# Up projection of a decoder layer: halo columns in four of seven Strassen parts, and the second half's halo read from the first half's result

## The chip, the cores and the metric

The kernel runs on one core of one Trainium2 chip. The metric is device time in microseconds (us) of one execution, from the first to the last instruction and what lies around them. Inside the core TensorE (PE) multiplies matrices, VectorE (DVE) and ScalarE (ACT) work on elements, GpSimd (POOL) is nearly unused here, and SyncE (SP) issues most DMAs. SBUF is the memory that the engines read, PSUM the one that TensorE writes its sums to.

## The reference

One layer of a hybrid decoder: 16 meta tokens and 1024 tokens, model width 1024, feed-forward width 2816. Attention and a convolution branch are merged, projected and normalized to `h`; then comes the convolutional feed-forward, which is where the change is:

```python
h  = layer_norm(DEEPNORM_ALPHA * h + mixed @ W_out)
up = causal_dwconv(h @ ffn_w_up, ffn_dw, ffn_dw_b)      # 1024 -> 2*2816, FFN_TAPS = 3
u, g = jnp.split(up, 2, axis=-1)
f  = (jax.nn.gelu(g, approximate=False) * u) @ ffn_w_down
h  = layer_norm(DEEPNORM_ALPHA * h + f)                 # meta tokens dropped
```

The convolution is causal with three taps, so each output token needs the up projection of its own token and of the two before it. A piece of tokens that is convolved by itself needs two columns more on its left: its halo.

## The kernel before, in words

**Stages.** Input projection, attention and convolution branch, merge, output projection (`out_rows`, which also normalizes `h` and turns it so that channels lie on partitions), up projection with convolution and gate, down projection. Every product is done in three terms, high part by high part, high by low and low by high, on operands split into two rounded fp32r halves. A split is two instructions: ACT casts to the high half, DVE subtracts to get the low half.

**The up projection as Strassen.** The 1024 tokens are cut into a first half (tokens 0 to 511) and a second half (512 to 1023), the 1024 input channels and the 2 x 2816 output channels also in two each. One product by halves is then seven products instead of eight, on seven sums of the inputs. In the order in which they are used these are B11, B21, BT2, BT4, BT1, BT3, B22. Each half of tokens is again done in two sub-halves of 256 columns: `sub` 0, whose operand has two more columns on its left, the halo, and `sub` 1. In `sub` 0 column 0 and 1 stand for tokens -2 and -1 in the first half, and for tokens 510 and 511 in the second. One part in one sub-half is 12 matmuls: four blocks `k` of 128 input channels by three terms. In `sub` 0 eight of the 12 are 260 columns wide (two columns of low halo, two of high halo, 256 tokens: the halo's low half lies ahead of its high half in the same row, so that a separate term isn't needed), the other four are 256 wide. In `sub` 1 all are 256 wide.

**The loop.** `for c in range(FC)` goes over 22 chunks of 128 + 128 output channels (the u side `c` and the gate side `FC + c`). The parts accumulate in four PSUM tiles: px, pz, px, pw, py, px, py for the seven parts in their order. After a part, `copy` (ACT) or `tt` (DVE) takes the bank to SBUF and forms the four Strassen results c11 and c12 (the gate's two token halves), c21 and c22 (u's two halves); u13 and u2 are intermediate sums. These are 516 columns wide: two columns of low halo product, two of high, 512 tokens. `conv_ffn` first adds the two halo products with two one-column activations on ACT, then convolves (one ACT instruction, two DVE instructions); `gelu` and `f_out` make the gate and store the product. Chunk 0 is done in two passes, `sub` 1 first and then `sub` 0, because the last rows of `h` come late: between the two passes `turn` transposes and evicts the last rows, and the sums of the parts of `sub` 0 (`form_t2`, `form_t3`, `form_t4`) and their splits (`bsplit` by `split_of`) are formed. `edges` puts the halo of both halves into the first two columns of each channel block of `h` in the tile FA, from the small tile `edge`, which `turn` fills.

**Order.** Each engine works its own queue in the order in which the instructions were given or ranked (`rank`, `after`, `line` pin some of them). Weights are loaded by SP, split by `wsplit` up to nine products ahead (`w_ahead(9)`), and kept in a ring in RHO and in the tiles `w`.

**Where operands lie.** Buffers come from pools on two sides of SBUF. `edge` is a tile of [128 partitions, 2, 8, 2] floats, 128 bytes in each partition, on the left side. The left buffers that are allocated behind it, each one where the last one ends, are among others the weight tiles `wr` and `w`, the tiles FA, RHC, RHO, OB and OA. RX, RW and OC lie on the right side. `B_AT` says where each part's operand is: in `sub` 0 B11 in RHC, B21 in RHO, BT2, BT1, BT3 and BT4 in OA, B22 in RX; in `sub` 1 B11, B21, BT2 and BT1 in OC, the others in RHC. The weights (the operand that TensorE holds) are in RHO and `w`, in this stage and in others, and the earlier stages pair the same left and right buffers.

Of the kernel before, what the change touches and what calls it, by code (L numbers as in the profile page):

```python
# [23 lines left out]
F = mybir.dt.float32  # L24
# [89 lines left out]
def tile_hybrid_layer(  # L114
# [24 lines left out]
    @contextmanager  # L139
    def rank(p):  # L140

        saved = tc.cur_priority
        tc.cur_priority = p
        yield
        tc.cur_priority = saved
# [1088 lines left out]
            [(OC, OC_UP + i * 2048, 0) for i in range(4)] + [(RHC, x + R_DN, 0) for x in (4096, 2048, 6144)]]  # L1234
    B11, B21, BT2, BT1, BT3, BT4, B22 = range(7)

    def bsum(sub, q, hl):
        r = row(sub, q, hl)
        return r[:, :, 2:260] if sub == 0 and not hl else r

    def row(sub, q, hl):
        t, o, back = B_AT[sub][q]
        hi = HP if sub == 0 else 256
        o += (4 * 256 if back and not hl else 4 * hi if hl and not back else 0)
        n = 256 if hl else hi
        return t[:, o:o + 4 * n].rearrange("p (k n) -> p k n", k=4)

    def bmat(sub, q, j, k):

        if sub:  # L1250
            return row(1, q, j % 2)[:, k]
        return row(0, q, j % 2)[:, k, 0:(260, 256, 260)[j]]

    lined, high = [], []
# [10 lines left out]
    def wide(x):  # L1265
        return x.rearrange("p (k n) -> p k n", k=4)
# [3 lines left out]

    def bsplit(sub, q, src, cs=slice(None)):
        with rank(RK_SUMS):
            src = wide(src)[:, :, cs]
            hi = bsum(sub, q, 0)[:, :, cs]
            ins = nc.scalar.copy(hi, src)
            if (sub, q) in ((0, BT2), (0, BT4), (0, BT1), (0, BT3)):
                if high:
                    after(ins, high[-1])
                high.append(ins)
            n = src.shape[2]  # L1280
            a = cs.start or 0
            x = 2 if sub == 0 and a == 0 else 0
            a -= 2 if sub == 0 and a else 0
            lo = bsum(sub, q, 1)[:, :, a:a + n - x]
            line(nc.vector.tensor_tensor(lo, src[:, :, x:], f32(hi)[:, :, x:], OP.subtract))
            if x:
                line(nc.vector.tensor_tensor(row(0, q, 0)[:, :, 0:2], src[:, :, :2], f32(hi)[:, :, :2], OP.subtract))
# [28 lines left out]


    WO_ORDER = (4, 5, 0, 1, 2, 3, 6, 7)
    edge = const.tile([P, 2, KC, 2], F, name="edge")
    r_next = [1]  # L1320

    def out_rows(i, between=(), work=()):
# [51 lines left out]
    def turn(i, r, n, ins, banks=None, behind=None, upper=False):  # L1374
        with rank(RK_TURN):
            for j, k0 in enumerate((4, 0) if upper else (0, 4)):
                ps = banks[j] if banks else pat.tile([P, 512], F, name="ps_h", tag="s", bufs=2)
                for k in range(4):
                    ins = nc.tensor.transpose(ps[:, k * P:(k + 1) * P], r[:, (k0 + k) * P:(k0 + k + 1) * P], ident)
                    if behind:  # L1380
                        after(ins, behind[-1])
                        behind.append(ins)
                for k in range(k0, k0 + 4):
                    src = ps[:, (k - k0) * P:(k - k0) * P + n]
                    if n < P:
                        dst = edge[:, 0, k]
                    else:
                        h, jj = divmod(i, 4)
                        sub = 0 if jj < 2 else 1
                        a = 2 + jj * P - SUB[sub][0]  # L1390
                        dst = h1F(sub, h, k)[:, a:a + P]
                    nc.scalar.activation(dst, src, AF.Identity, bias=b1col(k), scale=g1col(k))
                    if i == 3:
                        nc.scalar.activation(edge[:, 1, k], src[:, P - 2:P], AF.Identity, bias=b1col(k), scale=g1col(k))
        return behind[-1] if behind else None


# [68 lines left out]
            w_ahead(n)  # L1466

    def edges():
        for h in range(2):
            with rank(RK_TURN):  # L1470
                nc.vector.tensor_copy(FA[:, h * 2064:h * 2064 + 2064].rearrange("p (k n) -> p k n", n=258)[:, :, 0:2],
                                      edge[:, h])

    ahead = []
    work = {0: [(split_of, 1, B11), (split_of, 1, B21), (split_of, 1, B22)],
# [36 lines left out]
    c11, c21, u2 = (FA[:, 4128 + i * CU:4128 + (i + 1) * CU] for i in range(3))  # L1512
    c12, c22, u13 = (RT[:, i * CU:(i + 1) * CU] for i in range(3))

    def conv_ffn(cc, o):
        t = ftmp()
        for i in range(2):
            nc.scalar.activation(cc[:, 2 + i:3 + i], cc[:, 2 + i:3 + i], AF.Identity, bias=cc[:, i:i + 1], scale=1.0)
        cc = cc[:, 2:]
        nc.scalar.activation(t, cc[:, 2:HW], AF.Identity, bias=ffw(3, o), scale=ffw(2, o))  # L1520
        nc.vector.scalar_tensor_tensor(t, cc[:, 1:HW - 1], ffw(1, o), t, OP.mult, OP.add)
        nc.vector.scalar_tensor_tensor(t, cc[:, 0:HW - 2], ffw(0, o), t, OP.mult, OP.add)
        return t

    def gelu(t):
        nc.scalar.activation(t, t, AF.Gelu)
        return t

    def f_out(c, h, gate, t):
        nc.vector.tensor_tensor(t, t, gate, OP.mult)  # L1530
        f_stores.append(load(fd[c, :, h * 512:(h + 1) * 512], t))
# [39 lines left out]
    for c in range(FC):  # L1571
        V4, X, Z, Y = (pup.tile([P, 1024], F, name=n, tag=n) for n in ("pw", "px", "pz", "py"))
        passes = ((1,), (0,)) if c == 0 else ((0, 1),)
        for subs in passes:
            last = subs == passes[-1]
            w_next = iter(range(7))
            a, b = SUB[subs[0]][0] + (2 if subs[0] else 0), SUB[subs[-1]][1] + 2

            def at(t):
                return t[:, 252 + a:252 + b]  # L1580

            def prod(q, bank, first):
                if last:
                    w_ahead(9)
                    ah, al = w_ready.pop(0)
                else:
                    ah, al = w_ready[next(w_next)]
                for sub in subs:
                    terms = [(k, j) for k in range(4) for j in range(3)]
                    if sub == 0:  # L1590
                        terms = [(k, j) for j in (0, 2, 1) for k in range(4)]
                    for i, (k, j) in enumerate(terms):
                        o = bank[:, 512:768] if sub else bank[:, (252, 256, 252)[j]:512]
                        ins = nc.tensor.matmul(o, (ah, ah, al)[j][:, k * P:(k + 1) * P], bmat(sub, q, j, k),  # L1594
                                               start=first and i == 0, stop=i == 11, skip_group_check=not first)
                        if i == 0 and last_mm:
                            after(ins, last_mm[-1])
                    last_mm.append(ins)

            def tt(*x):  # L1600
                with rank(RK_CHAIN):
                    return nc.vector.tensor_tensor(*x)

            def copy(*x):
                with rank(RK_CHAIN):
                    copied.append(nc.scalar.copy(*x))  # L1606

            prod(B11, X, True)
            copy(u13[:, a:b], at(X))
            prod(B21, Z, True)  # L1610
            if last and c not in (0, FH + 1):
                sums_load(c - 1 if c <= FH else c - 2)
            tt(c11[:, a:b], at(Z), u13[:, a:b], OP.add)
            prod(BT2, X, False)
            copy(u2[:, a:b], at(X))
            if not last:
                turn(5, *last_rows, (V4, Z), last_mm, True)
                for q in (B11, B21):
                    split_of(0, q, LATE)
                form_t2(0, LATE)  # L1620
                formed.append(lined[-1])
                form_t4(0, LATE)
                form_t3(0, LATE)
                for q in (BT2, BT4, BT1, BT3, B22):
                    split_of(0, q)
            if last:
                g0 = gelu(conv_ffn(c11, FC + c))
            prod(BT4, V4, True)
            prod(BT1, Y, True)
            copy(c22[:, a:b], at(Y))  # L1630
            prod(BT3, X, False)
            copy(u13[:, a:b], at(X))
            ins = tt(c22[:, a:b], c22[:, a:b], u13[:, a:b], OP.add)
            if last and c not in (0, FH + 1):
                sums_form(c - 1 if c <= FH else c - 2, ins)
            tt(c21[:, a:b], u13[:, a:b], at(V4), OP.subtract)
            prod(B22, Y, False)
            tt(c12[:, a:b], at(Y), u2[:, a:b], OP.add)
            if last:
                f1 = conv_ffn(c22, c)  # L1640
                f_out(c, 0, g0, conv_ffn(c21, c))
                f_out(c, 1, gelu(conv_ffn(c12, FC + c)), f1)
    up_stack.close()


# [247 lines left out]
```

## Time and profile before

| what | value |
|---|---|
| median of 3 runs | 1254.46 us (1253.59, 1254.46, 1257.59) |
| span of the profiled execution | 1253.2 us, 23194 instructions |
| TensorE busy | 1239.1 us, 99% of the span |
| VectorE busy | 1078.1 us, 86% |
| ScalarE busy | 627.4 us, 50% |
| mean granted TensorE clock | 0.999 of full speed |
| DMA | 212.20 MB, mean 169 GB/s |

The execution's own time has no row beside its span in the page; the fastest run is 0.4 us above the span, the median 1.3 us. In the profile a line such as L1594 is a line of the kernel. A row of a timeline has start, duration, engine, line, operation, output and inputs, tile on the array, shape, and the count of equal instructions in a row. Matmuls overlap: one row's end lies after the next row's start, so durations of single matmuls are longer than their spacing, and what a group costs is read from start to start.

### The profile page before, as it was taken

The page shows a single profiled execution, that of the slowest core. Times are in us where ns is not written, and L with a number is a line of the kernel's source. Part 1 is how long each engine was busy: PE and PEld are TensorE (multiplying, and loading weights), DVE is VectorE, ACT ScalarE, POOL GpSimd, SP SyncE. Part 2 cuts the span into 40 slices and gives each one's busy share as a digit, 9 for nine tenths or more (in the row PEclk, how much of TensorE's full clock was granted, in tenths as well). Part 3 has the DMA queues.
Part 4 walks back from the last instruction along what each step waited for, and adds up shares of the span by engine and source line. Part 5 has one row for each costly group of instructions (what it writes and reads, how often), then busy time and mean ns, then how long its engine had stood idle before and what let it go on. Part 6 is the DMA issues. An engine that isn't in the chain of part 4 may idle for free.

```text
span 1253.2 us, 23194 instructions
## 1 busy us (share of the span) xinstructions
PE 1239.1 (99%) x9176; PEld 1173.8 (94%) x9176; DVE 1078.1 (86%) x1862; ACT 627.4 (50%) x1284; POOL 7.4 (1%) x8
## 2 busy tenths in 40 slices
PE   8999999999999999999999999999999999999997
PEld 7999999999999999788899999999999998888886
DVE  8989999999978677448899999998999977896697
ACT  8533255655474233344676556565565654545330
POOL 0000000001000000000000000000000000000000
PEclk9999999999999999999999999999999999999999
DMA  7383633432256564222145555453454567998712
GB/s 261 117 292 102 191 93 98 109 95 81 73 157 173 170 164 119 85 94 75 68 160 191 194 197 201 161 211 137 163 206 175 196 227 251 395 342 330 276 60 84
DMA packets 98687, 212.20 MB, mean 169 GB/s; under 512 B 11395, under 2 KB 38595, under 8 KB 98322
## 3 DMA queue, kind: packets, MB, share of 16 engines
q1 hardware_dynamic: 84414, 199.57, 46.9%
q10 hardware_dynamic: 14164, 11.15, 2.8%
q8 instruction: 72, 1.18, 0.4%
q14 instruction: 37, 0.30, 0.1%
HBM read 150.29 MB, written 62.70 MB: 170 GB/s over the span
## 4 chain that ended last, share of the span: by engine, by line
PE 96%; DVE 2%; ACT 1%; DMA 1%; issue 0%; SPq 0%; DVEq 0%; ACTq 0%
PE px L1594 15%; PE py L1594 10%; PE ps_x L1739 9%; PE ps_z L340 8%; PE ps_z L343 8%; PE ps_z L344 8%; PE ps_z L1739 7%; PE ps_p L1172 7%; PE pz L1594 5%; PE pw L1594 5%; PE ps_w L344 2%; PE ps_w L343 2%; PE ps_w L340 2%; PE ps_z L575 2%; PE ps_t L943 1%; PE ps_s L919 1%
## 5 line engine op out<-in xcount | busy, mean ns | idle before, releaser
L340 PE MATMUL ps_z<-RHO,w 128*128 128x256 f32 (+2 forms) x864 | 243.2, 281 | 0.0
L343 PE MATMUL ps_z<-RHO,w 128*128 128x256 f32 (+2 forms) x864 | 242.3, 280 | 0.0
L344 PE MATMUL ps_z<-RHC,w 128*128 128x256 f32 (+2 forms) x864 | 242.2, 280 | 0.0
L343 PEld LDWEIGHTS ps_z<-RHO,w 128*128 128x128 f32 x864 | 162.5, 188 | 0.5
L344 PEld LDWEIGHTS ps_z<-RHC,w 128*128 128x128 f32 x864 | 162.7, 188 | 0.2
L340 PEld LDWEIGHTS ps_z<-RHO,w 128*128 128x128 f32 x864 | 162.5, 188 | 0.1
L749 DVE SCALAR_TENSOR_TENSOR FA<-cin,cdw,FA 128x1026 f32<-128x1026 f32 x120 | 154.3, 1295 | 0.7
L300 ACT CAST w<-wr 128x1024 fp32r<-128x1024 f32 x37 | 38.8, 1048 | 64.0 <-PE ps_z L344 48.0
L1412 DVE TENSOR_TENSOR RHO<-wr,RHO 128x512 fp32r<-128x512 f32 x94 | 64.0, 684 | 3.6 <-ACT RHO L1411 3.5
L1411 ACT CAST RHO<-wr 128x512 fp32r<-128x512 f32 x94 | 56.9, 619 | 15.6 <-DVE wr L1429 7.9
L1429 DVE TENSOR_TENSOR wr<-wr 128x512 f32<-128x512 f32 x88 | 60.1, 683 | 0.1
L758 ACT ACTIVATE FA<-ps_z,colr 128x258 f32<-128x258 f32 (+1 forms) x64 | 30.1, 472 | 59.0 <-PE ps_z L344 50.7
L303 DVE TENSOR_TENSOR w<-wr,w 128x1024 fp32r<-128x1024 f32 x37 | 45.1, 1218 | 7.6 <-ACT w L300 7.4
L1606 ACT COPY FA<-px 128x516 f32<-128x516 f32 (+2 forms) x23 | 13.1, 571 | 71.2 <-PE px L1594 71.2
L1172 PE MATMUL ps_p<-OC,w 128*128 128x256 f32 (+1 forms) x384 | 48.1, 278 | 0.0
L1172 PE MATMUL ps_p<-OA,w 128*128 128x256 f32 (+1 forms) x384 | 47.8, 278 | 0.0
L1172 PEld LDWEIGHTS ps_p<-OC,w 128*128 128x128 f32 x384 | 46.2, 188 | 0.1
L1172 PEld LDWEIGHTS ps_p<-OA,w 128*128 128x128 f32 x384 | 45.9, 188 | 0.0
L1412 DVE TENSOR_TENSOR w<-wr,w 128x512 fp32r<-128x512 f32 x60 | 40.7, 684 | 4.7 <-ACT w L1411 4.7
L1594 PE MATMUL px<-OA,RHO 128*128 128x260 f32 x324 | 43.0, 282 | 0.0
L1594 PE MATMUL px<-OC,RHO 128*128 128x256 f32 x324 | 41.2, 276 | 0.8 <-DVE OB L1345 0.8
L1594 PE MATMUL px<-RHC,RHO 128*128 128x256 f32 (+1 forms) x312 | 40.6, 279 | 0.1
(457 smaller groups left out, 3109.3 us busy)
## 6 DMA issues: line engine op xcount, KB each, us to landing
wr<-in_w_up_dram SPq DMA_DIRECT2D x44, 512.0 KB, 3.6
wr<-in_w_z_dram SPq DMA_DIRECT2D x29, 512.0 KB, 4.2
OB<-in_w_down_dram SPq DMA_DIRECT2D x24, 512.0 KB, 5.2
fd<-FA SPq DMA_DIRECT2D x44, 256.0 KB, 2.0
FA<-sd SPq DMA_DIRECT2D x15, 512.0 KB, 8.9
qt<-qd SPq DMA_DIRECT2D x28, 256.0 KB, 4.1
OB<-td SPq DMA_DIRECT2D x14, 512.0 KB, 8.7
sgd<-FA ACTq DMA_DIRECT2D x48, 128.0 KB, 2.4
```

What stands on the lines that cost most here:

```text
L300: ins = nc.scalar.copy(hi, raw)
L303: return nc.vector.tensor_tensor(lo, raw, f32(hi), OP.subtract)
L340: ins = nc.tensor.matmul(ps, al, bh, start=i == 0, stop=False)
L343: nc.tensor.matmul(ps, ah, bh, start=False, stop=False)
L344: last = nc.tensor.matmul(ps, ah, bl, start=False, stop=i == n - 1)
L749: nc.vector.scalar_tensor_tensor(acc[c], cin[:, j:j + U], wc, acc[c], OP.mult, OP.add)
L1172: nc.tensor.matmul(ps[:, :b - a], x, rhs(k, hl, a, b), start=k + j == 0, stop=k == 3 and j == 2)
L1411: nc.scalar.copy(hi, src)
L1412: ins = nc.vector.tensor_tensor(lo, src, f32(hi), OP.subtract)
L1429: ins = nc.vector.tensor_tensor(*x)
L1594: ins = nc.tensor.matmul(o, (ah, ah, al)[j][:, k * P:(k + 1) * P], bmat(sub, q, j, k), start=first and i == 0, stop=i == 11, skip_group_ch ...
L1739: nc.tensor.matmul(banks[i], l[:, ts], r[:, ws], start=first and a and x + k == 0, stop=z and x == len(ops) - 1 and k == 2, skip_group_che ...
```

## The change

Four parts, B11, B21, BT3 and BT4, keep the halo in `sub` 0 (`HALO`). BT2, BT1 and B22 have none any more: all their 12 matmuls are 256 wide, in the order of `sub` 1's terms, on an operand without the halo in front. In Strassen's sums these three parts enter u2, c22 and c12. Hence u2, c22 and c12 are copied and added from column 4 on, and their halo columns are not computed at all: the convolution of c22 and c12 (second half of the tokens) gets its two halo columns by one ACT copy of the last two columns of c21 and c11 (first half), which are those very tokens. c11 and c21 (first half) still use the two activations, on products of parts with halo. For the four parts to give the first half's halo without the three others, `edges` now sets the halo of the four quadrants of `h` (by half and channel block) to E0, E1, E0 and 0, where E are the two edge tokens of the first half: the sums of the three dropped parts would be zero there. The second half's edge is not needed, so that `edge` is [P, KC, 2], 64 bytes in each partition, and the eight activations of `turn` that filled the other half are gone. The splits of the three parts cast 1024 columns instead of 1032, and lose their DVE subtraction of the halo's low part.

The diff (the line numbers of the profile are those of the kernel before; what stands below line 1234 moves by up to 14 lines):

```diff
+    HALO = (B11, B21, BT3, BT4)
+
     def bsum(sub, q, hl):
         r = row(sub, q, hl)
+        if sub == 0 and not hl and q not in HALO:
+            t, o, back = B_AT[0][q]
+            o += back * 1024
+            return t[:, o:o + 1024].rearrange("p (k n) -> p k n", k=4)
         return r[:, :, 2:260] if sub == 0 and not hl else r
...
         if sub:
             return row(1, q, j % 2)[:, k]
+        if q not in HALO:
+            return (row(0, q, 1) if j == 1 else bsum(0, q, 0))[:, k]
         return row(0, q, j % 2)[:, k, 0:(260, 256, 260)[j]]
...
     def bsplit(sub, q, src, cs=slice(None)):
         with rank(RK_SUMS):
-            src = wide(src)[:, :, cs]
+            whole = sub == 0 and q not in HALO
+            src = wide(src)[:, :, slice(2, None) if whole else cs]
...
-            x = 2 if sub == 0 and a == 0 else 0
+            x = 2 if sub == 0 and a == 0 and not whole else 0
...
-    edge = const.tile([P, 2, KC, 2], F, name="edge")
+    edge = const.tile([P, KC, 2], F, name="edge")
...
-                    if i == 3:
-                        nc.scalar.activation(edge[:, 1, k], src[:, P - 2:P], AF.Identity, bias=b1col(k), scale=g1col(k))
...
     def edges():
-        for h in range(2):
-            with rank(RK_TURN):
-                nc.vector.tensor_copy(FA[:, h * 2064:h * 2064 + 2064].rearrange("p (k n) -> p k n", n=258)[:, :, 0:2],
-                                      edge[:, h])
+        with rank(RK_TURN):
+            halo = FA[:, 0:2 * 2064].rearrange("p (k n) -> p k n", n=258)[:, :, 0:2]
+            nc.vector.tensor_copy(halo[:, 0:KC], edge)
+            nc.vector.tensor_copy(halo[:, KC:KC + 4], edge[:, 0:4])
+            nc.vector.memset(halo[:, KC + 4:], 0.0)
...
-    def conv_ffn(cc, o):
+    def conv_ffn(cc, o, before=None):
         t = ftmp()
-        for i in range(2):
-            nc.scalar.activation(cc[:, 2 + i:3 + i], cc[:, 2 + i:3 + i], AF.Identity, bias=cc[:, i:i + 1], scale=1.0)
+        if before is not None:
+            nc.scalar.copy(cc[:, 2:4], before[:, HW:CU])
+        else:
+            for i in range(2):
+                nc.scalar.activation(cc[:, 2 + i:3 + i], cc[:, 2 + i:3 + i], AF.Identity, bias=cc[:, i:i + 1],
+                                     scale=1.0)
...
-                    if sub == 0:
+                    if sub == 0 and q in HALO:
                         terms = [(k, j) for j in (0, 2, 1) for k in range(4)]
                     for i, (k, j) in enumerate(terms):
-                        o = bank[:, 512:768] if sub else bank[:, (252, 256, 252)[j]:512]
+                        o = bank[:, 512:768] if sub else bank[:, (252 if q in HALO and j != 1 else 256):512]
...
-            copy(u2[:, a:b], at(X))
+            copy(u2[:, m:b], at(X, m))
...
-            copy(c22[:, a:b], at(Y))
+            copy(c22[:, m:b], at(Y, m))
...
-            ins = tt(c22[:, a:b], c22[:, a:b], u13[:, a:b], OP.add)
+            ins = tt(c22[:, m:b], c22[:, m:b], u13[:, m:b], OP.add)
...
-            tt(c12[:, a:b], at(Y), u2[:, a:b], OP.add)
+            tt(c12[:, m:b], at(Y, m), u2[:, m:b], OP.add)
             if last:
-                f1 = conv_ffn(c22, c)
+                f1 = conv_ffn(c22, c, c21)
                 f_out(c, 0, g0, conv_ffn(c21, c))
-                f_out(c, 1, gelu(conv_ffn(c12, FC + c)), f1)
+                f_out(c, 1, gelu(conv_ffn(c12, FC + c, c11)), f1)
```

**TensorE in chunk 1, before.** The seven parts of `sub` 0 (260 wide, from RHC, RHO, OA, RX) take turns with those of `sub` 1 (256 wide, from OC and RHC); the first name is the PSUM tile, the names behind the arrow are where the two operands lie. Here stand BT2 to BT1 with the `sub` 1 groups between them.

```order
L1594 MATMUL px<-OA,RHO 128x260 x8
L1594 MATMUL px<-OA,RHO 128x256 x4
L1594 MATMUL px<-OC,RHO 128x256 x12
L1594 MATMUL pw<-OA,RHO 128x260 x8
L1594 MATMUL pw<-OA,RHO 128x256 x4
L1594 MATMUL pw<-RHC,RHO 128x256 x12
L1594 MATMUL py<-OA,RHO 128x260 x8
L1594 MATMUL py<-OA,RHO 128x256 x4
L1594 MATMUL py<-OC,RHO 128x256 x12
```

The same place of the changed kernel.

```order
L1608 MATMUL px<-OA,RHO 128x256 x12
L1608 MATMUL px<-OC,RHO 128x256 x12
L1608 MATMUL pw<-OA,RHO 128x260 x8
L1608 MATMUL pw<-OA,RHO 128x256 x4
L1608 MATMUL pw<-RHC,RHO 128x256 x12
L1608 MATMUL py<-OA,RHO 128x256 x12
L1608 MATMUL py<-OC,RHO 128x256 x12
```

BT2 (px) and BT1 (py) lose the eight wide matmuls, BT4 (pw) keeps them; the number of matmuls and their order among parts is the same.

**ScalarE between the two passes of chunk 0, before.** The last rows' transposes are evicted (L1392), then the parts of `sub` 0 are cast (L1275), with weight casts (L1411) and copies out of PSUM (L1606) among them.

```order
L1392 ACTIVATE FA<-pz,colr 128x128 x4
L1275 CAST RX<-FA 128x4x258
L1411 CAST w<-wr 128x512
L1411 CAST RHO<-wr 128x512
L1606 COPY OB<-py 128x256
L1275 CAST OA<-OB 128x4x258
L1411 CAST RHO<-wr 128x512
L1606 COPY OB<-px 128x256
L1275 CAST OA<-FA 128x4x258 x3
L1606 COPY OB<-px 128x260
```

The same place of the changed kernel.

```order
L1401 ACTIVATE FA<-pz,colr 128x128 x4
L1526 COPY OB<-FA 128x2
L1284 CAST RX<-FA 128x1024
L1418 CAST w<-wr 128x512
L1418 CAST RHO<-wr 128x512
L1620 COPY OB<-py 128x256
L1284 CAST OA<-OB 128x1024
L1418 CAST RHO<-wr 128x512
L1620 COPY OB<-px 128x256
L1284 CAST OA<-FA 128x4x258
L1284 CAST OA<-FA 128x1024
L1284 CAST OA<-FA 128x4x258
L1620 COPY OB<-px 128x260
```

The two-column copy of chunk 0's first halo (L1526, from c11 in FA to c12 in OB) now stands at the head of this stretch, since its source is ready from the first pass; three of the five casts are 8 columns narrower.

More of the change, by code (lines that the diff above doesn't have):

```diff
@@ L1385, in turn @@
                     if n < P:
-                        dst = edge[:, 0, k]
+                        dst = edge[:, k]
                     else:
@@ L1577, in tile_hybrid_layer, with at @@
             a, b = SUB[subs[0]][0] + (2 if subs[0] else 0), SUB[subs[-1]][1] + 2
-            def at(t):
+            m = max(a, 4)
+            def at(t, a=a):
                 return t[:, 252 + a:252 + b]
```

## The prediction

> **What bounds the kernel now.** I read the page's busy times and its chain of waits first, then the busy times by stage, then the timeline of TensorE through one chunk.
>
> ```profile
> PE 1239.1 (99%) x9176; PEld 1173.8 (94%) x9176; DVE 1078.1 (86%) x1862; ACT 627.4 (50%) x1284; POOL 7.4 (1%) x8
> PE 96%; DVE 2%; ACT 1%; DMA 1%; issue 0%; SPq 0%; DVEq 0%; ACTq 0%
> ```
>
> TensorE is busy for 99% of the span and makes 96% of the chain. By stage (stretch, length, then busy time of PE, weight load, DVE, ACT, POOL, granted clock, DMA share, GB/s):
>
> ```profile
> 602.00:640.00 38.00, 35.98 (x299) 34.86 (x298) 34.79 (x63) 25.58 (x53) 0.00 (x0) 1.00 0.22 80
> 640.00:1034.00 394.00, 394.00 (x3400) 394.00 (x3399) 363.74 (x578) 236.46 (x504) 0.00 (x0) 1.00 0.52 189
> ```
>
> The second row is the up projection's steady part: TensorE never idles, at clock 1.00. The first is its entry, where TensorE idles 38.00 - 35.98 = 2.0 us. So in the loop only a shorter or longer stream of matmuls moves the end, as long as DVE (394.00 - 363.74 = 30.3 us idle) and ACT keep up. One period of the stream, TensorE's timeline from BT1 (py) of one chunk to BT1 of the next:
>
> ```profile
> 773.70 1.58 PE L1594 MATMUL py<-OA,RHO 128*128 128x260 f32 x12
> 775.11 1.52 PE L1594 MATMUL py<-OC,RHO 128*128 128x256 f32 x12
> 776.47 1.59 PE L1594 MATMUL px<-OA,RHO 128*128 128x260 f32 x12
> ...
> 779.26 1.59 PE L1594 MATMUL py<-RX,RHO 128*128 128x260 f32 x12
> 780.69 1.52 PE L1594 MATMUL py<-RHC,RHO 128*128 128x256 f32 x12
> 782.05 1.59 PE L1594 MATMUL px<-RHC,RHO 128*128 128x260 f32 x12
> ...
> 787.62 1.59 PE L1594 MATMUL px<-OA,w 128*128 128x260 f32 x12
> 789.05 1.52 PE L1594 MATMUL px<-OC,w 128*128 128x256 f32 x12
> ...
> 793.18 0.40 PE L1594 MATMUL py<-OA,w 128*128 128x260 f32 x2
> ```
>
> Costs are read from start to start. A group of 12 with halo ("128x260") takes 775.11 - 773.70 = 1.41 us as BT1, 1.43 as B22 (780.69 - 779.26) and 1.43 as BT2 (789.05 - 787.62). A group of 12 at 256 takes 1.36 (776.47 - 775.11, 782.05 - 780.69), or 1.36 / 12 = 113.3 ns each.
>
> **The change, part by part.** *Narrower matmuls.* The three parts lose 0.05 + 0.07 + 0.07 = 0.19 us per chunk, on the path: 22 x 0.19 = 4.2 us gained, if they then run like the 256 wide groups of today. One rule speaks for less: the Trainium skill (TensorE: Matmul & The Clock Gate, Back-to-back issue gap) gives an isolated spacing of N / 2.4 + 2.5 ns, so four columns are 1.7 ns, and 24 matmuls in 22 chunks an estimated 0.9 us. The rows show four times that, since the wide groups cost more than their columns, and they decide.
>
> *Halo by copy.* Two pairs of one-column activations per chunk become two copies of two columns. Pairs on ACT's timeline:
>
> ```profile
> 627.24 0.48 ACT L1518 ACTIVATE OB<-OB 128x1 f32<-128x1 f32 x2
> 627.62 0.80 ACT L1520 ACTIVATE FA<-OB,coll 128x512 f32<-128x512 f32 x1
> ```
>
> A pair takes 627.62 - 627.24 = 0.38 us, so one instruction 0.19; ACT gains some 0.38 us per chunk. It is 40% idle in the steady stretch (236.46 of 394.00), so this is worth nothing. The copy for c22 waits for c21, and the one for c12 for c11. Those sums come one and many instructions earlier on the same DVE queue, and behind the waiting copies stand only convolutions whose results go out by DMA, so nothing that TensorE needs soon. The narrower copies and additions (512 for 516 columns) are too small to count.
>
> *Halo splits.* Three of the seven subtractions of L1287 go:
>
> ```profile
> 619.89 0.15 DVE L1287 TENSOR_TENSOR OA<-FA,OA 128x8 fp32r<-128x8 f32 x1
> 619.97 1.21 DVE L1285 TENSOR_TENSOR OA<-FA,OA 128x1024 fp32r<-128x1024 f32 x1
> ```
>
> 0.08 us from start to start, three times 0.24 us once in the kernel, on DVE between the two passes. The waits of TensorE there end on ACT, not on these, so I count nothing; at most it gains 0.24. The eight edge activations that go run earlier, under the output projection, and are hidden by it.
>
> *One instruction moved on ACT.* Between the passes of chunk 0 the copy of the halo columns of c12 comes ahead of the casts of the last parts. That place is a queue that TensorE waits for:
>
> ```profile
> 610.23 1.53 ACT L1392 ACTIVATE FA<-pz,colr 128x128 f32<-128x128 f32 x4
> 611.62 1.09 ACT L1275 CAST RX<-FA 128x1032 fp32r<-128x1032 f32 x1
> ...
> 613.60 0.42 ACT L1606 COPY OB<-py 128x256 f32<-128x256 f32 x1
> 613.87 1.11 ACT L1275 CAST OA<-OB 128x1032 fp32r<-128x1032 f32 x1
> ...
> 615.34 0.42 ACT L1606 COPY OB<-px 128x256 f32<-128x256 f32 x1
> 615.61 3.02 ACT L1275 CAST OA<-FA 128x1032 fp32r<-128x1032 f32 x3
> 618.48 0.43 ACT L1606 COPY OB<-px 128x260 f32<-128x260 f32 x1
> ```
>
> From 610.23 to 618.9 ACT has no gap. The two copies out of px, at 615.34 and 618.48, free the bank for the next part. TensorE (rows below) starts at 615.82, 1.73 us after the 12 of 614.09, which take 1.36, and at 618.96, right after the copy's end:
>
> ```profile
> 614.09 1.66 PE L1594 MATMUL py<-RHC,w 128*128 128x256 f32 x12
> 615.82 1.70 PE L1594 MATMUL px<-RHC,RHO 128*128 128x260 f32 x12
> 617.35 1.59 PE L1594 MATMUL pz<-RHO 128*128 128x260 f32 x12
> 618.96 1.71 PE L1594 MATMUL px<-OA,RHO 128*128 128x260 f32 x12
> ```
>
> An instruction of 0.19 us at the queue's head delays both by 0.19; since the first delay already shifts TensorE, it is paid once. The three casts lose 8 of 1032 columns, together some 0.02. I take +0.17; its ends are 0 (if the copy slips into an earlier gap) and 0.4 (if an instruction with a cold start takes the 0.3 to 0.4 us that a row shows from start to end and the second wait adds its own).
>
> *Sum of these.* -4.2 + 0.17 = -4.0 us. Against the profiled span of 1253.2 that is 1249.2; the median of the runs stands 1.3 above the span, so 1254.46 - 4.0 = 1250.4.
>
> *Addresses.* `edge` falls from 128 to 64 bytes, so all left buffers allocated behind it (`wr`, `w`, FA, RHC, RHO, OB, OA) move down by 64 bytes, while RX, RW and OC on the right stay. Each matmul that takes its moving columns from the right and its weights from the left gets another distance between its two addresses. In the up projection these are the 256 wide groups from OC (four parts) and B22's from RX: 5 x 12 = 60 per chunk, 1320 in all. Nothing in the trace of before shows that distance change. What it does show is that matmuls of the same shape and buffers run at two speeds (merge stage):
>
> ```profile
> 485.56 1.52 PE L1172 MATMUL ps_p<-OC,w 128*128 128x256 f32 x12
> 486.92 1.41 PE L1172 MATMUL ps_p<-OA,w 128*128 128x256 f32 x11
> ...
> 502.66 0.39 PE L344 MATMUL ps_w<-OA,RHC 128*128 128x512 f32 x1
> 502.89 2.99 PE L1172 MATMUL ps_p<-OC,w 128*128 128x256 f32 x24
> 505.71 0.40 PE L340 MATMUL ps_w<-OA,RHC 128*128 128x512 f32 x1
> ```
>
> Twelve from OC take 486.92 - 485.56 = 1.36 us, 113.3 ns each. Twenty-four a little later, behind 512 wide ones of another product, take 505.71 - 502.89 = 2.82, 117.5 ns each. No wait stands in these rows; TensorE just runs 4.2 ns slower per matmul and doesn't recover within 24. So matmul and weight load, both busy without a gap, can be in step or out of it, and the step depends on how the streams meet. I take it that the distance of the addresses is part of that. The price is bounded by 0 (no effect) and 4.2 ns on every matmul whose distance changes. Of the two ends I take the upper, since the row that shows a lost step is the only one here that prices it: 1320 x 4.2 = 5.5 us in this stage. In other stages the same holds for the merge's products from OC (the page's L1172 row of 384 of them: 1.6 us) and for some 600 matmuls of 512 columns that pair RX, RW or OC with left weights (by the same 4.2 ns 2.5 us, at the lower end 0). Sum: 5.5 + 1.6 + 2.5 = 9.6 us lost, against 4.0 gained: 1254.46 + 5.6 = 1260.1.
>
> **The rivals.** *A, the streams keep step.* The sum without the addresses: 1250.4, and faster. For it: every group of 256 in the period above, from OC, RHC, `w` or RHO, takes the same 1.36, although OC, RHC, `w` and RHO lie in different places; and the stream recovers from each wide group within the next one. Against it: those distances have been the same all through before, so the equality proves little, and the 117.5 exists. The Trainium skill (SBUF, Who interferes with whom) says that TensorE reads moving columns and weights through independent ports and never waits on anyone, which speaks for A: by it the addresses cost nothing. The two speeds of one and the same matmul above are not covered by that rule, and I take the rows as evidence that it isn't the whole.
>
> *B, a change of distance costs only its transition.* BT2, BT1 and B22 now have another spacing of rows (256 for 264 columns), and part follows part in other distances; each switch costs a few ns and then the stream is in step again. A wide group shows the size of such a switch: 8 matmuls of 260 with 4 of 256 cost 0.05 to 0.07 more than 12 of 256, of which the columns themselves explain 8 x (4 / 256) x 113.3 = 14 ns, so 36 to 56 ns for two switches, 18 to 28 each. With the 3 x 2 switches saved and, per chunk, 5 to 6 new ones, 5 x 18 to 6 x 28 ns, 2.0 to 3.7 us are given back in 22 chunks, and some more in the merge: 1252.4 to 1255, say 1254, no change that can be told.
>
> *D, ACT's queue decides.* If the copies for c22 and c12 made ACT wait long enough for the weights' casts behind them to come late, TensorE would stall in each chunk. TensorE idles nowhere in the steady stretch, and splits run up to nine products (about 9 x 2.8 us) ahead, so a wait of a few us is absorbed. It decides only when such a wait passes some 6 us per chunk, and the additions that the copies wait for come within one or two parts. From there each us more costs 22 us. I give it 2 in 100.
>
> The point from which C, the forecast, turns the sign: 4.0 us over the 2300 matmuls in question is 1.7 ns each. Below that the kernel is faster, at 3.4 ns it is slower by 0.3%.
>
> **How the numbers follow.** C (addresses lose the step) 0.48, A 0.34, B 0.16, D 0.02. A measurement of this kernel tells 0.3% from no change (its three runs lie within 0.32%), that is 1250.7 and 1258.2. C gives 1256 (a price half as high) to 1267 (all 136 matmuls of 256 columns of a chunk out of step: 22 x 76 x 4.2 = 7.0 us more); 1256 to 1258.2 is the same, about 0.08 of its 0.48. A gives 1249.4 (the wide groups' after-effects go too) to 1251, two thirds of it under 1250.7: faster 0.24, with 0.04 of B for 0.28. The same: 0.10 of A, 0.10 of B, 0.08 of C, 0.28. Slower: 0.40 of C, 0.02 of B, 0.02 of D, 0.44. The likeliest is C, 1260.1, its own range 1256 to 1267. The range over the cases is 1249.2 to 1266, which leaves out D, the worst of C and the best of A.
>
> **What would show it.** C: in the profile after, groups of 256 from OC take 1.41 us from start to start where those from RHC take 1.36, and merge rows from OC show 117.5. A: all groups of 256, BT2, BT1 and B22 among them, take 1.36, and a period is 19.48 - 0.19 = 19.29 us. B: 256 wide groups between 1.37 and 1.40, of all sources. The moved copy: the copies out of px end 0.17 later against the last eviction of the transposes, and TensorE's second wait with them. D: rows of TensorE with idle time in the steady stretch, ended by ACT. Wrong in any case would be a period above 19.9 us, or an idle TensorE there, or another granted clock.

## The result and the profile after

The changed kernel takes 1263.43 us (median; 1263.26 to 1266.32), the kernel before 1254.79 beside it. The ratio is 1.0076, 95% interval 1.0064 to 1.0087: slower by 0.8%. The forecast was slower, 1260.1 in a range of 1249.2 to 1266. The page's busy times and the engines of the chain of waits:

```profile
PE 1249.3 (99%) x9176; PEld 1181.6 (93%) x9176; DVE 1076.3 (85%) x1860; ACT 613.1 (48%) x1232; POOL 7.4 (1%) x8
PE 96%; DVE 2%; ACT 1%; DMA 1%; issue 0%; SPq 0%; DVEq 0%; ACTq 0%
```

TensorE has as many matmuls as before (9176), 3 parts x 8 x 22 = 528 of them four columns narrower, and is busy for 10.2 us more. DVE and ACT work less. The steady stretch of the up projection, columns as before (stretch, length, busy time of PE, weight load, DVE, ACT, POOL, clock, DMA share, GB/s):

```profile
640.00:1034.00 394.00, 394.00 (x3359) 394.00 (x3359) 361.64 (x577) 223.53 (x461) 0.00 (x0) 1.00 0.51 183
```

In the same 394 us TensorE still never idles, at the same clock, but comes to 3359 matmuls instead of 3400. Nothing waits, the stream itself is slower. TensorE's timeline in the changed kernel shows where:

```profile
773.23 1.58 PE L1608 MATMUL pz<-OC,w 128*128 128x256 f32 x12
774.65 1.58 PE L1608 MATMUL px<-OA,RHO 128*128 128x256 f32 x12
776.07 1.59 PE L1608 MATMUL px<-OC,RHO 128*128 128x256 f32 x12
777.49 1.60 PE L1608 MATMUL pw<-OA,RHO 128*128 128x260 f32 x12
778.93 1.53 PE L1608 MATMUL pw<-RHC,RHO 128*128 128x256 f32 x12
780.29 1.52 PE L1608 MATMUL py<-OA,RHO 128*128 128x256 f32 x12
781.65 1.58 PE L1608 MATMUL py<-OC,RHO 128*128 128x256 f32 x12
783.07 1.60 PE L1608 MATMUL px<-OA,RHO 128*128 128x260 f32 x12
...
785.87 1.60 PE L1608 MATMUL py<-RX,RHO 128*128 128x256 f32 x12
787.31 1.52 PE L1608 MATMUL py<-RHC,RHO 128*128 128x256 f32 x12
788.67 1.59 PE L1608 MATMUL px<-RHC,RHO 128*128 128x260 f32 x12
...
792.95 1.58 PE L1608 MATMUL pz<-OC,w 128*128 128x256 f32 x12
```

From start to start a group from OC takes 774.65 - 773.23 = 1.42 us, 783.07 - 781.65 = 1.42; before it was 1.36. A group from RHC still takes 1.36 (780.29 - 778.93, 788.67 - 787.31). Of the three parts that lost the halo only BT1 (py from OA) comes to 1.36; BT2 (px from OA) takes 776.07 - 774.65 = 1.42, hardly less than with the halo, and B22 (py from RX) 787.31 - 785.87 = 1.44, more than with it. The period is 792.95 - 773.23 = 19.72 us, before 19.48. The merge shows the same split by source, 1.42 us for 12 from OC, 118.3 ns each, and 1.26 for 11 from OA, 114.5; over the whole stage the 256 wide rows from OC go from 113.8 to 118.8 ns, and those from OA, which take turns with them, from 113.4 to 115.9:

```profile
489.00 1.58 PE L1172 MATMUL ps_p<-OC,w 128*128 128x256 f32 x12
490.42 1.43 PE L1172 MATMUL ps_p<-OA,w 128*128 128x256 f32 x11
491.68 1.58 PE L1172 MATMUL ps_p<-OC,w 128*128 128x256 f32 x12
```

Summed from start to start over all matmuls of a stage, after against before: merge 90.61 against 88.64 (+2.0), output projection 89.82 against 89.13 (+0.7), up projection 434.83 against 429.58 (+5.2), down projection 211.09 against 209.46 (+1.6), together 9.5 us. The rest of the difference of the two profiled spans (1264.5 - 1253.2 = 11.3) lies nearly all in the first stage, where matmuls wait for the first loads; that part differs between profiles whatever the kernel (one line's matmuls there, L518, take 9.3 to 11.9 us in the four profiles of the kernel before, the changed one and the first two experiments). The profile of the changed kernel is of its longest run (1266.32); the medians differ by 8.6.

### The profile page after: what moved, and what is told of

The parts are those of the page before. It is cut to its first block, busy times and chain, and to the rows that moved or that the text cites. A ratio compares the mean times of both kernels' runs of the same rounds, so it can differ in the third digit from the quotient of the medians.

```text
span 1264.5 us, 23150 instructions
## 1 busy us (share of the span) xinstructions
PE 1249.3 (99%) x9176; PEld 1181.6 (93%) x9176; DVE 1076.3 (85%) x1860; ACT 613.1 (48%) x1232; POOL 7.4 (1%) x8
## 4 chain that ended last, share of the span: by engine, by line
PE 96%; DVE 2%; ACT 1%; DMA 1%; issue 0%; SPq 0%; DVEq 0%; ACTq 0%
PE px L1608 15%; PE py L1608 9%; PE ps_x L1753 9%; PE ps_z L340 8%; PE ps_z L343 8%; PE ps_z L344 8%; PE ps_p L1172 7%; PE ps_z L1753 7%; PE pz L1608 5%; PE pw L1608 5%; PE ps_w L340 2%; PE ps_w L344 2%; PE ps_w L343 2%; PE ps_z L575 2%; PE ps_t L943 1%; PE ps_z L572 1%
## 5 line engine op out<-in xcount | busy, mean ns | idle before, releaser
L1620 ACT COPY FA<-px 128x512 f32<-128x512 f32 (+1 forms) x23 | 13.1, 568 | 81.0 <-PE px L1608 81.0
L1608 PE MATMUL px<-OA,RHO 128*128 128x256 f32 (+1 forms) x324 | 42.9, 281 | 0.0
L1532 ACT ACTIVATE FA<-OB,coll 128x512 f32<-128x512 f32 x44 | 35.8, 815 | 13.8 <-DVE OB L1616 13.8
```

## The experiments

**Take the address shift out of the change.** One line of the changed kernel:

```diff
-    edge = const.tile([P, KC, 2], F, name="edge")
+    edge = const.tile([P, 2, KC, 2], F, name="edge")[:, 0]
```

> The changed kernel, with the edge tile kept at 128 bytes (half of it unused), so that all buffers lie where they lay before; nothing else differs. Theory C (addresses): the groups of 256 from OC are back at 1.36 us from 1.42, the merge's rows from OC back at the spacing of before, and the whole comes to 1251 to 1253 us, faster than before. Rival (the narrower parts and their order disturb the stream wherever the buffers lie): OC groups stay at 1.42 and the time at 1262 to 1264.

Measured: 1253.78 us (11 runs), ratio 0.9993, interval 0.9984 to 1.0002. The slowdown is gone with 64 unused bytes. The profile (TensorE):

```profile
780.58 1.56 PE L1608 MATMUL py<-RX,RHO 128*128 128x256 f32 x12
781.98 1.53 PE L1608 MATMUL py<-RHC,RHO 128*128 128x256 f32 x12
...
787.55 1.52 PE L1608 MATMUL pz<-OC,w 128*128 128x256 f32 x12
788.91 1.56 PE L1608 MATMUL px<-OA,w 128*128 128x256 f32 x12
790.32 1.53 PE L1608 MATMUL px<-OC,w 128*128 128x256 f32 x12
```

OC is back at 1.36 (788.91 - 787.55). The time, though, is a little above the 1251 to 1253 that was expected: B22 takes 1.40 (781.98 - 780.58) and BT2 1.41 (790.32 - 788.91), not 1.36. So part of the gain from the narrower matmuls was still missing, and the interval allows no difference from before: the slowdown is gone, but the expected "faster" is not shown.

**The address shift alone.** The kernel before, with 16 floats of padding in a small tile ahead of the left buffers taken away, so that they lie 64 bytes lower, and no other edit:

```diff
-    coll = const.tile([P, n_kept - n_right + 24], F, name="coll")[:, :n_kept - n_right]
+    coll = const.tile([P, n_kept - n_right + 8], F, name="coll")[:, :n_kept - n_right]
```

> The kernel before, with 64 bytes of padding ahead of the left buffers taken away, so that they lie 64 bytes lower, as in the changed kernel; no instruction differs. Theory C: OC groups of 256 go from 1.36 to 1.42 (4 x 22 x 0.06 = 5.3 us), the merge loses 2 us, the other stages some 2, together 1263 to 1266 us. Rival (addresses don't matter): 1254 to 1256, all groups as before.

Measured: 1265.69 us, ratio 1.0090, interval 1.0075 to 1.0106. Not one instruction differs from the kernel before. By the starts of the matmuls the OC groups take 1.42 us in all 21 full chunks (1421 ns on average), the merge is at 90.61 us as in the changed kernel, and the up projection 7.1 us longer. The address shift alone is enough for the whole slowdown. By the sums of the starts the up projection loses 7.1 us with it and 5.2 with the change, so the narrower matmuls gave 1.8 back; the intervals of the two ratios overlap.

**What the spacing depends on.** Matmuls alone, in place of the layer:

```python
for wi in range(8):
    for mi in range(8):
        run(f"n_{LET[mi]}{LET[wi]}", mi * 8, wi * 8, 256, 256, 3)   # start of moving columns, of weights; width, spacing of rows, repeats
...
```

> A kernel of matmuls alone, which leaves the whole layer out: streams of 36 matmuls 256 wide, fp32r, with the order of terms of one part, for each of 8 x 8 pairs of start addresses of moving columns and weights (steps of 32 bytes, letters a to h), then 260 wide ones in the halo's row spacing, then 512 wide ones. Theory C: the spacing depends on the distance of the two addresses; some pairs at 113.3 ns, some at 117 to 120, and pairs of the same distance agree. Rival: 113.3 ns for all 64 pairs.

Measured, mean spacing of the last 12 of each 36, by the distance "address of the weights minus address of the moving columns, modulo 256 bytes" (eight pairs for each, the first pair at 0 bytes, n_aa, 119.4, ran while the stream started):

| distance, bytes | 0 | 32 | 64 | 96 | 128 | 160 | 192 | 224 |
|---|---|---|---|---|---|---|---|---|
| 256 wide, ns | 119.4 to 120.0 | 118.4 to 118.7 | 113.3 (one: 117.8) | 117.1 to 119.0 | 118.2 to 118.8 | 120.0 | 117.8 | 117.8 |
| 512 wide, ns | 227.2 to 230.6 | 232.5 to 232.8 | 232.5 to 233.3 | 233.7 to 234.6 | 232.8 to 233.6 | 233.0 to 234.5 | 228.5 to 229.7 | 233.2 to 233.5 |

From 60 to 480 us of that kernel VectorE, ScalarE and GpSimd do nothing, and the granted clock is 1.00. The 260 wide streams in the halo's row spacing, in which the distance moves on by 32 bytes with every block, come to 119.2 to 121.1 ns at all eight starts. Four neighbouring streams on its timeline, second letter the weights, first letter the moving columns, each letter 32 bytes on:

```profile
67.10 4.39 PE L40 MATMUL n_gb<-M,W 128*128 128x256 f32 x36
71.33 4.28 PE L40 MATMUL n_hb<-M,W 128*128 128x256 f32 x36
75.44 4.40 PE L40 MATMUL n_ac<-M,W 128*128 128x256 f32 x36
79.68 4.42 PE L40 MATMUL n_bc<-M,W 128*128 128x256 f32 x36
```

n_hb (distance 64 modulo 256) takes 75.44 - 71.33 = 4.11 us, n_gb (96) 4.23, and n_ac 4.24, although its distance is 64 as well: it is the one exception, taken up below. The rival, 113.3 for all pairs, falls. In the kernel before, the addresses that its program assigns give 64 for all groups of 256 in merge and up projection, and 0 for the 512 wide matmuls of output and down projection: the best place of each row of the table. In the changed kernel, the OC groups are at 0, the merge's OC products too, BT2's high half is at 192 and B22's at 128 (with the edge tile at 128 bytes, both at 192), and more than half of the down projection at 64 or 192.

**Put every narrow part at 64 bytes.** The changed kernel with the edge tile at 128 bytes, and, in the function `bsum`:

```diff
-            o += back * 1024
+            o += 1024 if back else 32
```

> The changed kernel with the edge tile at 128 bytes, and the high halves of BT2 and B22 in the first sub-half 128 bytes further on inside their own room, so that their distance to the weights is 64 bytes (mod 256) too. Theory C (the distance sets the spacing, 64 bytes is the one good one for 256 columns): BT2 and B22 go from 1.41 and 1.40 to 1.36, a chunk is 0.19 us shorter than before, and the whole comes to 1250 to 1251 us, 0.3% faster than before. Rival (the shift back was all that addresses do, the rest of the missing gain is the price of the new order of terms): 1253 to 1254, as with the edge tile alone.

Measured: 1250.72 us, ratio 0.9969, interval 0.9957 to 0.9980: faster than both kernels. TensorE's timeline:

```profile
773.60 1.52 PE L1608 MATMUL py<-OC,RHO 128*128 128x256 f32 x12
...
777.75 1.52 PE L1608 MATMUL py<-RX,RHO 128*128 128x256 f32 x12
779.11 1.52 PE L1608 MATMUL py<-RHC,RHO 128*128 128x256 f32 x12
...
786.04 1.52 PE L1608 MATMUL px<-OA,w 128*128 128x256 f32 x12
787.40 1.52 PE L1608 MATMUL px<-OC,w 128*128 128x256 f32 x12
...
792.89 1.52 PE L1608 MATMUL py<-OC,w 128*128 128x256 f32 x12
```

B22 and BT2 take 1.36 each, and the period is 792.89 - 773.60 = 19.29 us, 0.19 less than before. One stall of the steady stretch takes 0.5 us back: ACT waits for a load of weights, and behind it the copy out of px comes late (first row ACT, second TensorE). Behind the stall BT2 and the OC group after it, both at 64 bytes, run at 117 to 118 ns a matmul instead of 113.3, up to the next part with halo, so that with the slower groups it costs 0.8. The kernel with the edge tile alone stalls in the same chunk behind the same wait, for 0.3 us:

```profile
744.31 1.14 ACT L1418 CAST w<-wr 128x512 fp32r<-128x512 f32 x2 [2.32 <-DMA wr<-in_w_up_dram]
747.22 1.68 PE L1608 MATMUL px<-OA,RHO 128*128 128x256 f32 x12 [0.36 <-ACT OB L1620]
```

**Distance or place.** The changed kernel with its edge tile of 64 bytes, and the right side's buffers 64 bytes lower as well:

```diff
-    colr = constr.tile([P, n_right], F, name="colr")
+    colr = constr.tile([P, n_right + 16], F, name="colr")[:, :n_right]
```

> The changed kernel as it is, with 64 bytes taken off in front of the right side's buffers too, so that RX, RW and OC move by as much as the left ones and every distance between left and right is as before. Theory C (the distance counts, not the place): OC groups at 1.36, the whole as with the edge tile at 128 bytes, 1253 to 1254 us. Rival (the left buffers' own place counts): as the changed kernel, 1263 to 1264.

Measured: 1252.09 us, ratio 0.9983, interval 0.9973 to 0.9992. OC groups 1.36, B22 and BT2 1.40, merge 88.64 us as before. It is the distance between the two operands, not the place of either. The time is 0.9 us under the 1253 to 1254 that was expected, and some 1.7 under the kernel with the edge tile alone; the intervals of those two overlap.

**Finer steps and other widths.** Matmuls alone again:

```python
for s in range(24):
    run("s_" + "abcdefghijklmnopqrstuvwx"[s], 8 + s, 32, 256, 256, 3)
for tag, n, rows in (("t", 258, 320), ("u", 260, 320), ("v", 272, 320), ("x", 384, 384)):
    for mi in range(8):
        ps = run(f"{tag}_{LET[mi]}", mi * 8, 0, n, rows, 3)
```

> Matmuls alone again, without the layer. First 24 streams 256 wide whose moving address goes on by 4 bytes from stream to stream, s_a to s_x, from 96 bytes below the weights to 4 below (the weights 128 bytes above a multiple of 256): theory C expects 113.3 ns only around 64 bytes, s_i, and 117 to 120 away from it; whether the good place is one address or a range of 32 bytes is open. Then 258, 260, 272 and 384 wide streams at eight distances in steps of 32 bytes, with a row spacing that keeps the distance: C expects one good distance for each width, not the same for all. Rival: a flat row for each width.

```profile
53.03 4.44 PE L40 MATMUL s_h<-M,W 128*128 128x256 f32 x36
57.31 4.26 PE L40 MATMUL s_i<-M,W 128*128 128x256 f32 x36
61.41 4.54 PE L40 MATMUL s_j<-M,W 128*128 128x256 f32 x36
65.79 4.49 PE L40 MATMUL s_k<-M,W 128*128 128x256 f32 x36
```

Settled, s_i (64 bytes) runs at 113.3 ns; s_h (68 bytes) at 118.8, s_j (60 bytes) at 121.7, and none of the other 21 under 116.7. In steps of 4 bytes the good place is one address, not a range. By width, lowest to highest over the eight distances: 258 wide 118.6 to 121.2, 260 wide 118.7 to 121.1, 272 wide 123.3 to 126.7, 384 wide 173.3 to 176.7. So the expectation of one good distance for each width was wrong: 258 and 260 have none among the eight that comes near 113.3 (a place between the steps of 32 bytes was not tried), and 384 has five that are equal.

**From the matmuls alone back into the kernel.** Two edits of the kernel before, in `B_AT`: the four parts in OC moved inside OC, first by one float, then by eight.

```diff
-            [(OC, OC_UP + i * 2048, 0) for i in range(4)] + [(RHC, x + R_DN, 0) for x in (4096, 2048, 6144)]]
+            [(OC, OC_UP + 1 + i * 2048, 0) for i in range(4)] + [(RHC, x + R_DN, 0) for x in (4096, 2048, 6144)]]
```

> The kernel before, with the four parts that lie in OC (second sub-half) moved by 4 bytes inside OC; every instruction is the same and in the same order. Theory C, with the price read from the stream s_j of the matmuls alone (121.7 ns at 60 bytes of distance, against 113.3 at 64): the OC groups take 1.46 us instead of 1.36, 4 x 22 x 12 x 8.4 ns = 8.9 us, 1263 us. Rival (a shift matters only in steps of 32 or 64 bytes, or the matmuls alone don't carry over to the kernel): 1254 to 1255.

> The same with 32 bytes for 4. Theory C, with the price from the stream n_ab and its like (118.7 ns at 32 bytes of distance): OC groups at 1.42, 4 x 22 x 12 x 5.4 ns = 5.7 us, 1260 us, so less than for 4 bytes. Rival (the farther from the good place the worse): more than for 4 bytes.

Measured: 1265.96 us, ratio 1.0074 (interval 1.0054 to 1.0095), for 4 bytes, 3 us over the expected 1263; 1260.09 us, ratio 1.0039 (1.0026 to 1.0052), for 32 bytes, as expected. First the groups at 4 bytes, then at 32:

```profile
775.04 1.62 PE L1594 MATMUL px<-OC,RHO 128*128 128x256 f32 x12
776.50 1.59 PE L1594 MATMUL pw<-OA,RHO 128*128 128x260 f32 x12
777.92 1.52 PE L1594 MATMUL pw<-RHC,RHO 128*128 128x256 f32 x12
```

```profile
777.22 1.58 PE L1594 MATMUL py<-OC,RHO 128*128 128x256 f32 x12
778.63 1.59 PE L1594 MATMUL px<-OA,RHO 128*128 128x260 f32 x12
```

An OC group takes 776.50 - 775.04 = 1.46 us at 4 bytes (expected 1.46) and 778.63 - 777.22 = 1.41 at 32 (expected 1.42). One float costs more than eight, as in the matmuls alone. The sum of the up projection's matmuls is 9.8 and 5.6 us longer than before (expected 8.9 and 5.7).

**Does the past count?** Streams of 72 at the good distance, each behind another kind:

```python
for i, (n, rows, w) in enumerate(((512, 512, 0), (512, 512, 16), (384, 384, 16), (272, 320, 16), (260, 264, 16),
                                  (258, 320, 16), (256, 256, 0), (256, 256, 8))):
    for j, count in enumerate((1, 2)):
        run("p_" + LET[i] + "gh"[j], 0, w, n, rows, count)
        run("q_" + LET[i] + "gh"[j], 0, 16, 256, 256, 6)     # 256 wide at 64 bytes
```

> Matmuls alone, without the layer: streams of 72 matmuls 256 wide at the good distance of 64 bytes (q_), each behind 12 or 24 matmuls of another kind (p_): 512 wide at distance 0 and 64, 384, 272, 260, 258 wide, 256 wide at distance 0 and 32. If the distance alone sets the spacing, every q_ stream comes to 113.3 ns within a dozen matmuls, whatever stood ahead. If the past also counts, as the merge's 24 at 117.5 ns of the kernel before suggest, some of them, above all those behind 512 wide ones, stay at 117 to 118.

```profile
65.56 8.33 PE L40 MATMUL q_bh<-M,W 128*128 128x256 f32 x72
73.72 2.24 PE L40 MATMUL p_cg<-M,W 128*128 128x384 f32 x12
...
130.49 8.64 PE L40 MATMUL q_eh<-M,W 128*128 128x256 f32 x72
138.97 1.60 PE L40 MATMUL p_fg<-M,W 128*128 128x258 f32 x12
```

Behind 512 wide ones at 64 bytes, 384 and 258 wide ones the stream runs at 113.3 (73.72 - 65.56 = 8.16 us for 72); behind 512 wide ones at distance 0, 272, 260 wide ones and 256 wide ones at distances 0 and 32 it runs at 117.8 (138.97 - 130.49 = 8.48), to its end. Each kind gives the same speed behind 12 and behind 24 of it. So at 64 bytes there are two steady speeds, and the past picks one. The merge row of the prediction fits this: 24 at 117.5 ns, at distance 64, behind 512 wide ones at distance 0. So does the stall above, behind which two groups at 64 bytes ran at 117 to 118. The exception n_ac shows the same second speed, but it stands behind a stream at distance 64, a kind that was not tried here, and what picked its speed stays open.

## Why the prediction was right, and where its sizes were off

The forecast rested on the step *Addresses*: that the smaller edge tile moves the left buffers against the right ones, and that a matmul whose distance to its weights changes loses 4.2 ns. That holds by the two runs that separate it (64 bytes back: the loss is gone; 64 bytes alone: the loss is there without any other edit) and by the sign named ahead, OC groups at 1.41 where those from RHC take 1.36 (measured 1.42 and 1.36). The evidence that the prediction had for the step was weaker than the step. Its merge row of 24 at 117.5 ns lies at distance 64 like the rows at 113.3, and shows the second speed of one and the same distance; as the prediction itself says, nothing in the trace of before shows a change of distance. That the distance matters was a guess, with a chance of 0.48, which the runs bore out, and that 4.2 ns came near the 5.1 which a matmul from OC lost on average was luck. Period and idle time stayed within what was given as a limit (19.72 under 19.9, no idle time, clock 1.00).

Term by term against the measured:

- *Narrower matmuls*, 4.2 us gained: this is the term that was mis-sized most. BT1 gave its 53 ns per chunk, 1.2 us in all. BT2 gave 9 ns instead of 66, 1.3 us short. The step took for granted that the three parts run like the 256 wide groups of before; but BT2's unpadded high half came to lie at distance 192, with both operands on the left side, where the edge tile's size doesn't matter. Of the 57 ns that it misses per chunk, 43 are still missing with the edge tile back at 128 bytes (BT2 at 1403 ns by the starts); the other 14 go with the shift of its neighbours. The run with the halves placed at 64 bytes shows the whole 0.19 us per chunk.
- *Addresses* in the up projection, 60 x 4.2 ns per chunk. B22's share of it (50 ns) would have left it 16 ns better than with the halo; it lost 14, 0.7 us short. The four OC groups lost 245 ns per chunk where 48 x 4.2 = 202 were forecast, 1.0 us short: 4.2 ns came from a row that, as it turned out, shows the second speed of distance 64, while the settled loss at distance 0 is 120.0 - 113.3 = 6.7 ns, of which the first matmuls of each group are spared a part.
- Not in the sum: the groups with halo that follow a group at another distance. BT4 takes 27 ns more, B21 and BT3 6 each, 0.9 us in all.
- *Merge* 1.6: measured 2.0. It was counted as 384 products from OC, of which 96 are 258 wide and lost nothing; the 288 of 256 lost 1.4 us, and 0.7 came from the 288 from OA, which the sum didn't have. *512 wide matmuls* 2.5: measured 0.7 in the output and 1.6 in the down projection, 2.3.
- *One instruction moved on ACT*, +0.17: in the profile after the copy takes 0.08 us from start to start, and from the first group behind the transposes to the second wait's end it is 623.74 - 614.62 = 9.12 us against 9.06 before: 0.06.

```profile
614.62 1.65 PE L1608 MATMUL pw<-RHC,RHO 128*128 128x256 f32 x12 [1.16 <-ACT FA L1401]
623.74 1.69 PE L1608 MATMUL px<-OA,RHO 128*128 128x256 f32 x12
616.33 0.23 ACT L1526 COPY OB<-FA 128x2 f32<-128x2 f32 x1
616.41 1.09 ACT L1284 CAST RX<-FA 128x1024 fp32r<-128x1024 f32 x1
```

So 1260.1 was 3.3 us under the measured 1263.43: 1.3 from BT2, 1.0 from OC, 0.9 from the groups with halo, 0.7 from B22, together 3.9, and small terms of both signs.

Rival A, 1250.4, is what the change is worth once all 256 wide matmuls of the up projection stand at 64 bytes: 1250.72. Its argument, that groups of 256 from four places all took 1.36, was true of the rows, and the objection noted there, that all those distances were equal, was the reason. The rule of the Trainium skill quoted for it (SBUF, Who interferes with whom: independent ports, TensorE waits on no one) doesn't cover this: in the matmuls alone no other engine works, and the spacing still changes with the distance. Here the measurement decides. Rival B, a loss in the transitions only, falls: at the wrong distance the last 12 of 36 still take 117 to 120 ns. Rival D's sign, an idle TensorE behind ACT in the steady stretch, appeared in one chunk of the placed kernel and of the one with the edge tile alone, and not in the changed kernel; but ACT waited there for a load of weights, not in a copy for c22 or c12, as D has it.

## What to carry to other kernels

Where TensorE is the bound, compare a change with a variant that keeps all buffers at their old addresses before judging it: here 64 unused bytes decide between 0.8% slower and no change, and the right place for two operands between that and 0.3% faster. A change of the size of any small, early tile moves all that is allocated behind it, so pad it to the old size, or read the distance of moving operand and weights for the costliest matmuls. A loss of this kind shows as a longer spacing of equal matmuls by source buffer, with no wait in any view.

## What the runs showed of the hardware

- The spacing of fp32r matmuls of 256 columns in a stream with a new weight load for each depends on the distance of the addresses of weights and moving columns modulo 256 bytes: 113.3 ns at 64 bytes (or 117.8, next point), 116.7 to 123.3 elsewhere, and 4 bytes off is enough (118.8, 121.7). For 512 columns the lowest were 227.2 to 230.6 at distance 0 and 228.5 to 229.7 at 192, against 232.5 to 234.6 at the other six.
- At 64 bytes there are two steady speeds, 113.3 and 117.8, and for the eight kinds tried what ran just before picked one; it then held for 72 matmuls.
- 258 and 260 columns showed, at eight distances in steps of 32 bytes, none under 118.6 ns, so against the best of 256 the first two columns more cost 5 ns, where by proportion they would be 0.9.

Why the distance matters, what in the chip the two reads share, was not tried and stays open; so does how the past picks the speed.
